# Reciprocal roots as a power on GpSimd, stores on other queues, loads in another order: one trunk layer on one core

## The chip, the cores and the metric

The kernel runs on one core of a Trainium2 chip. The metric is device time in microseconds for one execution. TensorE (PE) multiplies matrices, and PEld is its loading of stationary operands; VectorE (DVE), ScalarE (ACT) and GpSimd (POOL) do the elementwise work; SyncE (SP) issues most of the transfers between HBM and the on-chip memory. Each engine runs its own instructions in order, and engines wait for each other by semaphores.

## The reference

One layer of a gated decoder trunk, for a prompt of 1024 tokens and for 8 samples of 8 tokens (64 tokens), which share all weights. The width is 1024, all data are float32.

```python
mod = silu(c) @ ada_w + ada_b
shift, scale, gate = split(mod, 3)
h = rmsnorm(x, norm_g) * (1 + scale) + shift
z = h @ w_in + b_in                  # 1024 -> 8456 columns, split for three branches
ya = chunk_gmlp(a_u, a_v)            # branch A: rmsnorm of a_v, 128-position mixing matrices
yb = swa_branch(b_q, b_k, b_v)       # branch B: rmsnorm of q and k, window attention with sinks
yc = mlstm_branch(c_qk, c_v, ...)    # branch C: causal conv, 4 heads, chunked scan, rmsnorm of each head
merged = sum over branches of sigmoid(m_g) * ((y * silu(g)) @ w_branch)
out = x + gate * (merged @ w_out)
```

Here `rmsnorm(x, g) = x * rsqrt(mean(x*x) + 1e-6) * g`. Beside the output, the new states of branches B and C (keys, values, conv rows, the matrices C, the vectors n and m) and the normalised rows of branch A are returned.

## The kernel before, in words

Both groups of tokens are handled together as 1088 columns (prompt first, then samples), in nine tiles of 128 tokens (the last has 64) or in three chunks of 384, 384 and 320. Each float32 product is made of three matmuls on a high and a low half (`hh`, `hl`) of either operand; the halves are made by ACT (a cast) and DVE (the difference). Weights come in slabs `hl` of two halves: four pieces are loaded by SP into three buffers `raw`, cast by ACT (line 124), and subtracted by DVE (line 125), in `load_pieces`; the next slab is loaded while one is used.

The program runs through these stages, in microseconds from the span's start:

- 0 to about 90: the adaLN columns (`mod`, weights `adaraw`, results `modA` and `modB`), the root mean square of each token tile (`norm1`), the transposed and modulated activations (`hprep`), and the first products. The string LOADS sets the order of the loads on SP: x are token tiles, a the adaLN weights, w the first slab, s seven rows of biases and gains. STEPS sets the order of the work: N norms, M `mod`, S the transposed rows of s, three digits a range of `hprep` with its products, P the pieces of the next slab.
- 90 to 360: branch C, one head after the other (`head`), interleaved with gate products. A head ends with its numerator `num` scaled by a reciprocal root of nine columns (lines 744 to 752), and with stores of C from `Cst` and `Cs`.
- 360 to 612: branch B and the start of A. PE's order is written out by hand here (a manual schedule with a list of steps and filler products); other engines are ordered by the scheduler. `k_norm`, `q_stats` and `q_transpose` normalise keys and queries; `kst` and `qraw` are key and query tiles, `Sm` scores.
- 612 to 1114: the gate and branch products of half the width each, as seven products instead of eight (Strassen-like). `raw_load` brings weights, `comb` adds or subtracts them, `prod` holds their halves (lines 1372 to 1378); `t_first`, `t_second`, `t_third` and `t_in_place` make the sums of activations. Gate columns of adaLN (`graw`, line 1628) are loaded along the way.
- 1114 to 1224: the output projection; its moving operand is the weight (`wo`, the first group `prod`), its stationary one the merged activations (`mh`, `ml`).

The reciprocal root is made on DVE: an integer shift and a multiply-add for a first guess, then three Newton steps of three instructions each (`rsqrt`, lines 160 to 168); for the nine token tiles a form of two instructions each step stands in `norm1` (lines 328 to 337). Elsewhere a scaling by the number of elements stands ahead of it.

Instructions of the same engine are put in order by a scheduler that follows the program's order and priorities. SP issues loads and stores in one queue; a store or load whose semaphore isn't there yet holds what is behind it. A load also waits for an earlier one on its lane, of which there are eight.

Of the kernel before, what the change touches and what calls it, by code (L numbers as in the profile page):

```python
# [11 lines left out]
I32 = mybir.dt.int32  # L12
MAGIC = 1597463007.0
# [26 lines left out]
def trunk_kernel(ctx: ExitStack, tc: tile.TileContext, I, O):  # L40
# [12 lines left out]
    hp = ctx.enter_context(tc.tile_pool(name="hact", bufs=1))  # L53
    sp = ctx.enter_context(tc.tile_pool(name="slots", bufs=1))
# [61 lines left out]
    def load_pieces(i):  # L116
        hl = wp.tile([128, 2, 2112], F32R, tag="hl", bufs=2, name="hl")
        off = 0
        for src in [x[:, j:j + x.shape[1] // 2] for x in specs[i] for j in (0, x.shape[1] // 2)]:
# [35 lines left out]
    rsc = ct([128, 2], "rsc")  # L155
    onecol = ct([128, 1], "onecol")
    V.memset(rsc[:, 0:1], -1.0)
    V.memset(rsc[:, 1:2], MAGIC)

    def rsqrt(y, x):  # L160
        p, n = x.shape[0], x.shape[1]
        t = cp.tile([128, 20], F32, tag="rst", bufs=2, name="rst")[:p, :n]
        V.tensor_scalar(y.bitcast(I32), x.bitcast(I32), 1, None, ALU.logical_shift_right)
        V.tensor_scalar(y.bitcast(I32), y.bitcast(I32), rsc[:p, 0:1], rsc[:p, 1:2], ALU.mult, ALU.add)
        for _ in range(3):
            V.tensor_tensor(t, y, y, ALU.mult)
            V.scalar_tensor_tensor(t, t, -0.5, x, ALU.mult, ALU.mult)
            V.scalar_tensor_tensor(y, t, 1.5, y, ALU.add, ALU.mult)
# [73 lines left out]
    with tc.tile_pool(name="start", bufs=1, side="right", reuse_waits="tile") as st:  # L242
# [81 lines left out]
        def norm1(n):  # L324
            tn = TILES[n][1]
            junk = st.tile([128, 1024], F32, name="junk")
            S.activation(junk[:tn], xt[n][:tn], AF.Square, accum_out=ss[:tn, n:n + 1])
            s, y = ss[:, n:n + 1], rst[:, n:n + 1]
            V.tensor_scalar(s, s, 1.0 / 1024, EPS, ALU.mult, ALU.add)
            V.tensor_scalar(y.bitcast(I32), s.bitcast(I32), 1, None, ALU.logical_shift_right)  # L330
            V.tensor_scalar(y.bitcast(I32), y.bitcast(I32), rsc[:, 0:1], rsc[:, 1:2], ALU.mult, ALU.add)
            V.tensor_scalar(s, s, -0.5, None, ALU.mult)
            t = st.tile([128, 1], F32, tag="rs1", bufs=4, name="rs1")
            for _ in range(3):
                V.scalar_tensor_tensor(t, y, y, s, ALU.mult, ALU.mult)
                V.scalar_tensor_tensor(y, t, 1.5, y, ALU.add, ALU.mult)
            V.tensor_scalar(xt[n][:tn], xt[n][:tn], y[:tn], None, ALU.mult)

        def norm(g):
# [9 lines left out]
            V.tensor_scalar(ss[:, sl], ss[:, sl], 1.0 / 1024, EPS, ALU.mult, ALU.add)  # L349
            rsqrt(rst[:, sl], ss[:, sl])  # L350
# [5 lines left out]
        for i in (64, 96):  # L356
            V.tensor_tensor(sel, sel, ident[:, i:i + 9], ALU.add)

        def mod(j):
# [15 lines left out]
            for d in range(2):  # L375
                k = 2 * j + d
                V.tensor_scalar(modA[:, k], pc[:, 16 * d:16 * d + 9], cols[:, CADA + 8 + k:CADA + 9 + k],
# [41 lines left out]
        for step in STEPS.split():  # L419
            if step == "P":  # L420
                load_pieces(1)
# [39 lines left out]
    with tc.tile_pool(name="cph", bufs=1, side="right", reuse_waits="tile") as c1:  # L461
# [166 lines left out]
        def head(h):  # L628
# [75 lines left out]
            nc.sync.dma_start(O["C_p"][0, 0, h], Cp[:, 0:128])  # L704
# [14 lines left out]
            for b2 in range(2):  # L719
# [12 lines left out]
                nc.sync.dma_start(O["C_s"][0, bs_, h].rearrange("b d e -> d b e"), Cs[b2][:, :, 0:128])  # L732
# [15 lines left out]
            V.tensor_scalar(r2, r2, 1.0 / 128, EPS, ALU.mult, ALU.add)  # L748
            r3 = c1.tile([128, 9], F32, tag="r3", name="r3")
            rsqrt(r3, r2)  # L750
# [29 lines left out]
        nc.sync.dma_start(O["n_p"].rearrange("a b h d -> (a b h) d"), nrowo[0:4])  # L780
        nc.sync.dma_start(O["n_s"].rearrange("a b h d -> (a b h) d"), nrowo[4:36])
# [1001 lines left out]
```

## Time and profile before

| what | value |
|---|---|
| three runs | 1227.0, 1229.13 and 1229.74 us; median 1229.13 |
| profiled execution | 1225.66 us, of which the span of the profile is 1223.9 |
| mean granted clock of TensorE | 0.98 |
| instructions of DVE, of POOL | 2146, 32 |
| DMA traffic | 129.76 MB, mean 106 GB/s |

Times in the profile are from the span's start. A row of a timeline gives start, duration, engine, line, operation, tiles and shapes, and in brackets the idle time just before and what ended it. In the chain of waits a row is one link: start, duration, engine and line. SPq, DVEq and PEq are the engines' queues, "issue" is time that nothing shown explains. A matmul's duration is modelled and overlaps with the next one's, so the distance between two starts says how fast they follow each other. Matmuls are named by moving and stationary operand.

### The profile page before, as it was taken

The page shows a single profiled execution, that of the slowest core. Times are in us where ns is not written, and L with a number is a line of the kernel's source. Part 1 is how long each engine was busy: PE and PEld are TensorE (multiplying, and loading weights), DVE is VectorE, ACT ScalarE, POOL GpSimd, SP SyncE. Part 2 cuts the span into 40 slices and gives each one's busy share as a digit, 9 for nine tenths or more (in the row PEclk, how much of TensorE's full clock was granted, in tenths as well). Part 3 has the DMA queues.
Part 4 walks back from the last instruction along what each step waited for, and adds up shares of the span by engine and source line. Part 5 has one row for each costly group of instructions (what it writes and reads, how often), then busy time and mean ns, then how long its engine had stood idle before and what let it go on. Part 6 is the DMA issues. An engine that isn't in the chain of part 4 may idle for free.

```text
span 1223.9 us, 23322 instructions
## 1 busy us (share of the span) xinstructions
PE 1173.7 (96%) x8900; PEld 1124.1 (92%) x8900; DVE 820.3 (67%) x2146; ACT 485.8 (40%) x1215; POOL 17.8 (1%) x32
## 2 busy tenths in 40 slices
PE   5899999999979999999979999999999999999998
PEld 2689999999969998988878999999999999999998
DVE  4767878655568778886599885655766676668333
ACT  4443444433332266887234433333433342236000
POOL 1000000000001000000000000000000000000000
PEclk9999999999989999999979999999999999999999
DMA  9711222224122211211144246522633364466332
GB/s 328 242 47 36 72 74 70 76 86 126 54 58 67 56 40 44 67 38 59 55 119 118 75 120 201 161 80 84 177 112 110 110 171 125 126 197 190 95 91 83
DMA packets 155818, 129.76 MB, mean 106 GB/s; under 512 B 13551, under 2 KB 146311, under 8 KB 155690
## 3 DMA queue, kind: packets, MB, share of 16 engines
q1 hardware_dynamic: 155706, 128.27, 35.4%
q8 instruction: 70, 1.15, 0.4%
q14 instruction: 42, 0.34, 0.1%
HBM read 99.39 MB, written 29.82 MB: 106 GB/s over the span
## 4 chain that ended last, share of the span: by engine, by line
PE 88%; DVE 5%; SPq 3%; DMA 3%; ACT 1%; issue 1%; DVEq 0%
PE pg L85 48%; PE pk L85 23%; PE pu L85 14%; PE pk L89 2%; DMA raw<-in_w_in_dram 2%; SPq L256 1%; PE pu L89 1%; DMA xts<-in_x_sample_dram 1%; SPq L272 1%; DVE comb L1372 0%; DVE prod L1378 0%; DVE hl L125 0%; ACT hl L124 0%; DVE wo L1378 0%; DVE ml L1585 0%
## 5 line engine op out<-in xcount | busy, mean ns | idle before, releaser
L85 PE MATMUL pg<-hl,hl 128*128 128x256 f32 (+3 forms) x904 | 281.1, 311 | 0.0
L85 PE MATMUL pg<-hh,hl 128*128 128x384 f32 (+1 forms) x912 | 242.2, 340 | 1.1 <-DVE hh L399 1.1
L85 PE MATMUL pg<-hl,hh 128*128 128x256 f32 (+1 forms) x1008 | 182.9, 287 | 1.0 <-DVE zif L524 1.0
L85 PEld LDWEIGHTS pg<-hl,hl 128*128 128x128 f32 x904 | 172.1, 190 | 2.4 <-issue 1.9
L85 PEld LDWEIGHTS pg<-hh,hl 128*128 128x128 f32 x912 | 163.8, 191 | 5.3 <-DVE hh L399 2.2
L85 PEld LDWEIGHTS pg<-hl,hh 128*128 128x128 f32 x1008 | 152.9, 190 | 1.5 <-PE pg L85 1.1
L1377 ACT CAST prod<-raw 128x512 fp32r<-128x512 f32 x76 | 47.1, 620 | 125.7 <-PE pk L85 54.8
L85 PE MATMUL pg<-hh,prod 128*128 128x272 f32 x400 | 84.9, 292 | 6.8 <-ACT prod L1377 6.8
L85 PE MATMUL pk<-hh,prod 128*128 128x272 f32 x368 | 78.0, 291 | 0.0
L85 PEld LDWEIGHTS pg<-hh,prod 128*128 128x128 f32 x400 | 66.7, 191 | 7.3 <-ACT prod L1377 6.9
L1378 DVE TENSOR_TENSOR prod<-raw,prod 128x512 fp32r<-128x512 f32 x76 | 52.0, 686 | 25.2 <-ACT prod L1377 24.9
L1377 ACT CAST prod<-comb 128x512 fp32r<-128x512 f32 x64 | 39.4, 616 | 69.3 <-PE pk L85 29.5
L1502 ACT ACTIVATE tt<-tt,bh 128x272 f32<-128x272 f32 x96 | 49.9, 522 | 41.0 <-DVE tt L1475 15.8
L85 PEld LDWEIGHTS pk<-hh,prod 128*128 128x128 f32 x368 | 61.4, 191 | 1.3 <-issue 0.4
L85 PE MATMUL pk<-tc,prod 128*128 128x272 f32 x444 | 61.5, 287 | 0.0
L85 PE MATMUL pg<-yh,prod 128*128 128x272 f32 x288 | 60.0, 287 | 0.0
L85 PE MATMUL pk<-yh,prod 128*128 128x272 f32 x288 | 59.9, 287 | 0.0
L85 PEld LDWEIGHTS pk<-tc,prod 128*128 128x128 f32 x444 | 57.6, 188 | 0.9 <-DVE tt L1544 0.4
L85 PE MATMUL pg<-hl,prod 128*128 128x272 f32 x200 | 58.1, 291 | 0.0
L85 PE MATMUL pg<-tc,prod 128*128 128x272 f32 x408 | 56.5, 287 | 0.0
L85 PE MATMUL pk<-hl,prod 128*128 128x272 f32 x184 | 53.5, 291 | 0.4 <-DVE hl L825 0.4
L85 PE MATMUL pu<-hh,prod 128*128 128x272 f32 x256 | 53.5, 289 | 0.0
(521 smaller groups left out, 2626.1 us busy)
## 6 DMA issues: line engine op xcount, KB each, us to landing
raw<-in_w_in_dram SPq DMA_DIRECT2D x124, 256.0 KB
dmg<-tt SPq DMA_DIRECT2D x88, 136.0 KB
mprev<-dmg SPq DMA_DIRECT2D x64, 136.0 KB
adaraw<-in_ada_w_dram SPq DMA_DIRECT2D x16, 512.0 KB
stage<-dy SPq DMA_DIRECT2D x24, 272.0 KB
xt<-in_x_prompt_dram SPq DMA_DIRECT2D x8, 512.0 KB
graw<-in_ada_w_dram SPq DMA_DIRECT2D x16, 256.0 KB
raw<-in_w_out_dram SPq DMA_DIRECT2D x32, 128.0 KB
```

The source lines that it names most:

```text
L85: T.matmul(out, lhsT=lhsT, rhs=rhs, start=start, stop=stop)
L89: T.transpose(out, in_, ident[:k, :k])
L256: nc.sync.dma_start(raw.rearrange("p (k c) -> p k c", k=4), kv(ada_w[:, base:base + 256])[:, 4 * (q % 2):4 * (q % 2) + 4])
L272: nc.sync.dma_start(xx[:TILES[n][1]], x_p[128 * n:128 * n + 128] if n < 8 else x_s)
L1377: S.copy(t[:, 0], x)
L1378: V.tensor_tensor(t[:, 1], x, t[:, 0].bitcast(F32), ALU.subtract)
L1502: S.activation(x, x, AF.Tanh, bias=bh[:, b:b + 1], scale=0.5)
```

## The change

It does the following.

1. The reciprocal root is made by GpSimd in two instructions: a scaling with an added epsilon, and a power with exponent -0.5 (`rsqrt`). This replaces the sequence on DVE and the scaling ahead of it, for the nine token tiles, the four heads of branch C, three calls for keys, six for queries and one for branch A.
2. Stores of C, n, the conv rows, the branch C outputs (`dy<-hn`), the gates of branch B (`dsg<-zb`) and the rows of A go to GpSimd's queue; the twenty stores of attention outputs (`dy<-yo`, `dy<-ys`) to ScalarE's. They were on SP.
3. At the start the last adaLN weights (a3) are loaded ahead of the rows (s), M3 stands ahead of S, the next slab's pieces are issued after the last `modA`, and the fourth piece has a buffer of its own (`raw1`).
4. The last query tile is scaled in `q_stats` instead of `q_transpose`.
5. `t_first` moves ahead in the program and to other slots (m4, m5); gate loads `graw` are issued after the newest weight load; the `comb` buffers move to a pool of their own.
6. Two unused tiles of 64 bytes per partition shift what is allocated behind them. Together with smaller constants, the activations' tiles move down by 192 bytes, the slots and slabs by 128, and raw and prod tiles of the Strassen-like stage go elsewhere.

```diff
 LEAD = 5
-LOADS = "x0 r x1 x2 a0 w0 a1 w1 x3 x4 x5 a2 x6 x7 x8 s a3"
-STEPS = "N0 M0 010 M1 230 N1 M2 450 011 231 451 N2 S M3 670 012 671 232 452 672 P"
+LOADS = "x0 r x1 x2 a0 w0 a1 w1 x3 x4 x5 a2 x6 x7 x8 a3 s"
+STEPS = "N0 M0 010 M1 230 N1 M2 450 011 231 451 N2 M3 S 670 012 671 232 452 672 P"
...
+    ctx.enter_context(tc.tile_pool(name="shift", bufs=1)).tile([128, 16], F32, name="shift")
     sp = ctx.enter_context(tc.tile_pool(name="slots", bufs=1))
...
-            raw = wp.tile([128, 528], F32, tag="raw", bufs=3, name="raw")
+            raw = raws[q] if raws[q] is not None else wp.tile([128, 528], F32, tag="raw", bufs=3, name="raw")
...
-    rsc = ct([128, 2], "rsc")
-    V.memset(rsc[:, 0:1], -1.0)
-    V.memset(rsc[:, 1:2], MAGIC)
-
-    def rsqrt(y, x):
+    mhalf = ct([128, 1], "mhalf")
+    V.memset(mhalf, -0.5)
+
+    def rsqrt(y, x, count):
         p, n = x.shape[0], x.shape[1]
-        t = cp.tile([128, 20], F32, tag="rst", bufs=2, name="rst")[:p, :n]
-        V.tensor_scalar(y.bitcast(I32), x.bitcast(I32), 1, None, ALU.logical_shift_right)
-        V.tensor_scalar(y.bitcast(I32), y.bitcast(I32), rsc[:p, 0:1], rsc[:p, 1:2], ALU.mult, ALU.add)
-        for _ in range(3):
-            V.tensor_tensor(t, y, y, ALU.mult)
-            V.scalar_tensor_tensor(t, t, -0.5, x, ALU.mult, ALU.mult)
-            V.scalar_tensor_tensor(y, t, 1.5, y, ALU.add, ALU.mult)
+        G.tensor_scalar(x, x, 1.0 / count, EPS, ALU.mult, ALU.add)
+        G.tensor_tensor(y, x, mhalf[:p].broadcast_to([p, n]), ALU.pow)
...
             if step == "P":
-                load_pieces(1)
+                with tc.issue_after(last["m"].ins):
+                    load_pieces(1, [None] * 3 + [st.tile([128, 528], F32, name="raw1")])
...
-            nc.sync.dma_start(O["C_p"][0, 0, h], Cp[:, 0:128])
+            nc.gpsimd.dma_start(O["C_p"][0, 0, h], Cp[:, 0:128])
...
-            nc.sync.dma_start(dy[0, h], hn[h])
+            nc.gpsimd.dma_start(dy[0, h], hn[h])
...
-            V.tensor_scalar(rf, rf, 1.0 / 64, EPS, ALU.mult, ALU.add)
             r3 = bt([128, 3, 4], "r3", bufs=2)
-            rsqrt(r3.rearrange("p n h -> p (n h)"), rf)
+            rsqrt(r3.rearrange("p n h -> p (n h)"), rf, 64)
             r3s[g] = r3
+            if n0 == 6:
+                for i in range(2):
+                    qr = qraw[g][i][:64, 8].rearrange("p (h d) -> p h d", d=64)
+                    V.tensor_tensor(qr, qr, r3[:64, 2, 2 * i:2 * i + 2].unsqueeze(2).broadcast_to([64, 2, 64]), ALU.mult)
...
-                nc.sync.dma_start(dy[1, 2 * g:2 * g + 2, :, 128 * n:128 * n + 128].rearrange("f p t -> p f t"),
+                nc.scalar.dma_start(dy[1, 2 * g:2 * g + 2, :, 128 * n:128 * n + 128].rearrange("f p t -> p f t"),
...
-                nc.sync.dma_start(dsg[f, :, c0:c0 + n], z)
+                nc.gpsimd.dma_start(dsg[f, :, c0:c0 + n], z)
...
-            t = slot(("m2", "m3")[k % 2], [128, 2, HT], name="tx")
+            t = slot(("m4", "m5")[k % 2], [128, 2, HT], name="tx")
...
-        tail = {11: lambda: t_second(0), 13: lambda: t_second(1), 17: lambda: t_second(2),
+        tail = {0: lambda: t_first(0), 1: lambda: t_first(1), 2: lambda: t_first(2), 3: lambda: t_first(3), 11: lambda: t_second(0), 13: lambda: t_second(1), 17: lambda: t_second(2),
...
+    w3 = ctx.enter_context(tc.tile_pool(name="w3", bufs=1, reuse_waits="tile"))
+    w3.tile([128, 16], F32, name="shift")
...
-        nc.sync.dma_start(r.rearrange("p (k c) -> p k c", k=src.shape[1]), src)
+        newest[0] = nc.sync.dma_start(r.rearrange("p (k c) -> p k c", k=src.shape[1]), src).ins
...
-        r = w2.tile([128, 512], F32, tag="comb", bufs=3, name="comb")
+        r = w3.tile([128, 512], F32, tag="comb", bufs=3, name="comb")
...
-                nc.sync.dma_start(raw.rearrange("p (k c) -> p k c", k=2),
-                                  kv(ada_w[:, 2048 + 256 * g:2304 + 256 * g])[:, 2 * q:2 * q + 2])
+                with tc.issue_after(newest[0]):
+                    nc.sync.dma_start(raw.rearrange("p (k c) -> p k c", k=2),
+                                      kv(ada_w[:, 2048 + 256 * g:2304 + 256 * g])[:, 2 * q:2 * q + 2])
```

The other calls of `rsqrt` and the other stores change in the same way. Three places show the order. First, DVE at the start. Before, with the slab's pieces `hl<-raw`, the scaling of the sample tokens `xts`, and the adaLN columns:

```order
L337 TENSOR_SCALAR xt<-xt,rstd 128x1024
L336 SCALAR_TENSOR_TENSOR rstd<-rs_590,rstd 128x1
L335 SCALAR_TENSOR_TENSOR rs_590<-rstd,ss 128x1
L336 SCALAR_TENSOR_TENSOR rstd<-rs_590,rstd 128x1
L125 TENSOR_TENSOR hl<-raw,hl 128x528
L337 TENSOR_SCALAR xts<-xts,rstd 64x1024
L377 TENSOR_SCALAR modA<-pk,cols 128x9
L379 TENSOR_SCALAR modB<-pk,cols 128x9
L377 TENSOR_SCALAR modA<-pk,cols 128x9
L379 TENSOR_SCALAR modB<-pk,cols 128x9
```

Now:

```order
L388 TENSOR_TENSOR hl_404<-hf,hh_403 128x384
L365 TENSOR_SCALAR modA<-pk,cols 128x9
L367 TENSOR_SCALAR modB<-pk,cols 128x9
L365 TENSOR_SCALAR modA<-pk,cols 128x9
L367 TENSOR_SCALAR modB<-pk,cols 128x9
L414 COPY cols<-pk 128x52
L415 COPY cols<-pk 128x16
L124 TENSOR_TENSOR hl<-raw,hl 128x528 x3
L124 TENSOR_TENSOR hl<-raw_731,hl 128x528
```

The adaLN columns and, ten rows further ahead (row 48 of this engine), the scaling of xts stand ahead of all four pieces, one of which is in a buffer of its own.

Second, DVE at the end of branch C's last head, up to the scaling of `num`. `tc` and `tx` belong to the sums of activations for the Strassen-like stage, `rst` and `r` to the reciprocal root. Before:

```order
L125 TENSOR_TENSOR hl<-raw,hl 128x512
L166 TENSOR_TENSOR rst<-r_2986 128x9
L167 SCALAR_TENSOR_TENSOR rst<-rst,r_2982 128x9
L825 TENSOR_TENSOR tc<-tx,tc 128x544
L168 SCALAR_TENSOR_TENSOR r_2986<-rst,r_2986 128x9
L125 TENSOR_TENSOR hl<-raw,hl 128x512
L976 MEMSET qraw 64x128
L166 TENSOR_TENSOR rst<-r_2986 128x9
L167 SCALAR_TENSOR_TENSOR rst<-rst,r_2982 128x9
L168 SCALAR_TENSOR_TENSOR r_2986<-rst,r_2986 128x9
L751 TENSOR_TENSOR r_2982<-r_2986,dd 128x9
L752 TENSOR_TENSOR num<-num,r_2982 128x9x128
```

Now:

```order
L719 TENSOR_TENSOR Cs<-Cs,pk 128x4x128
L813 TENSOR_TENSOR tc<-tx,tc 128x544
L1208 TENSOR_TENSOR tx<-tx 128x544
L1206 TENSOR_TENSOR tx<-hh_312 128x544
L124 TENSOR_TENSOR hl<-raw,hl 128x512
L1207 TENSOR_TENSOR tx<-hl_313 128x544
L124 TENSOR_TENSOR hl<-raw,hl 128x512
L739 TENSOR_TENSOR r_2871<-r_2874,dd 128x9
L124 TENSOR_TENSOR hl<-raw,hl 128x512
L813 TENSOR_TENSOR tc<-tx,tc 128x544
L1208 TENSOR_TENSOR tx<-tx 128x544
L740 TENSOR_TENSOR num<-num,r_2871 128x9x128
```

The Newton steps are gone. From the second `Cs` to `num` stand nine large instructions (`tc`, `tx` and `hl`) and the small product r. Before, the slab's fourth piece is the last `hl` shown; now it stands behind `num`.

Third, SP at the beginning of the Strassen-like stage. Before:

```order
L1181 DMA dsg<-zb 128x384 x2
L1165 DMA dy<-ys 128x2x32 x2
L1181 DMA dsg<-zb 128x320
L1165 DMA dy<-ys 128x2x32
L1628 DMA graw<-in_ada_w_dram 128x2x256 x3
L1367 DMA raw_7314<-in_w_in_dram 128x4x128
L1367 DMA raw_7316<-in_w_in_dram 128x4x128
L1367 DMA raw_7318<-in_w_in_dram 128x4x128
L1628 DMA graw<-in_ada_w_dram 128x2x256
L1367 DMA raw_7320<-in_w_in_dram 128x4x128
L1367 DMA raw_7367<-in_w_in_dram 128x4x128
```

Now:

```order
L1236 DMA WT<-dWT 128x512
L1242 DMA vgb<-in_gmlp_vnorm_g_dram 64x512
L1238 DMA bsb<-in_gmlp_bs_dram 128x512
L1355 DMA raw_7086<-in_w_in_dram 128x4x128
L1355 DMA raw_7088<-in_w_in_dram 128x4x128
L1355 DMA raw_7090<-in_w_in_dram 128x4x128
L1355 DMA raw_7092<-in_w_in_dram 128x4x128
L1355 DMA raw_7139<-in_w_in_dram 128x4x128
L1355 DMA raw_7141<-in_w_in_dram 128x4x128
L1355 DMA raw_7143<-in_w_in_dram 128x4x128
L1355 DMA raw_7145<-in_w_in_dram 128x4x128
L1617 DMA graw<-in_ada_w_dram 128x2x256 x4
```

The eight weight loads stand ahead of the gate loads, and the stores of dsg and dy are on other queues.

More of the change, by code (lines that the diff above doesn't have):

```diff
@@ L327, in norm1 @@
             S.activation(junk[:tn], xt[n][:tn], AF.Square, accum_out=ss[:tn, n:n + 1])
[L328 to L336, printed above, removed]
+            y = rst[:, n:n + 1]
+            rsqrt(y, ss[:, n:n + 1], 1024)
             V.tensor_scalar(xt[n][:tn], xt[n][:tn], y[:tn], None, ALU.mult)
@@ L348, in norm @@
                 S.activation(junk[:tn], xt[n][:tn], AF.Square, accum_out=ss[:tn, n:n + 1])
-            V.tensor_scalar(ss[:, sl], ss[:, sl], 1.0 / 1024, EPS, ALU.mult, ALU.add)
-            rsqrt(rst[:, sl], ss[:, sl])
+            rsqrt(rst[:, sl], ss[:, sl], 1024)
             for n in range(3 * g, 3 * g + 3):
@@ L357, in trunk_kernel @@
             V.tensor_tensor(sel, sel, ident[:, i:i + 9], ALU.add)
+        last = {}
         def mod(j):
```

37 lines of the change are left out of this document (14 added, 23 removed).

## The prediction

> **What bounds the kernel now.** I read the page first (engine shares, then the chain of waits), then PE's own waits, then the stretches in which these fall, each by the timeline of the engine that is waited for.
>
> ```profile
> PE 1173.7 (96%) x8900; PEld 1124.1 (92%) x8900; DVE 820.3 (67%) x2146; ACT 485.8 (40%) x1215; POOL 17.8 (1%) x32
> PE 88%; DVE 5%; SPq 3%; DMA 3%; ACT 1%; issue 1%; DVEq 0%
> ```
>
> PE is busy for 1173.7 of 1223.9 us and makes 88% of the chain that ended last. So no removed DVE, SP or Pool time is worth anything by itself; it is worth what it takes from PE's idle time, from the half-clock time behind an idle stretch, or from the time of a matmul. PE's waits, largest first (us in all, times, longest):
>
> ```profile
> PE pk L89 <- DVE num L752: 8.7, 1, 8.7
> PE pg L85 <- ACT prod L1377: 6.8, 1, 6.8
> PE pk L89 <- DVE ff L543: 2.9, 1, 2.9
> PE pk L89 <- ACT kst L958: 2.3, 1, 2.3
> PE pk L89 <- DVE qraw L1007: 2.0, 1, 2.0
> PE pu L89 <- ACT Sm L1064: 1.4, 1, 1.4
> ```
>
> These add up to 24.1 us, and each stands at a place that the change touches; elsewhere nothing can be gained but by faster matmuls. Two stretches, from the start and from attention, have their uses below (columns: stretch, its length, busy time and count of PE, PEld, DVE, ACT, POOL, granted clock, DMA share, GB/s).
>
> ```profile
> 34.00:38.00 4.00, 2.60 (x26) 1.69 (x22) 2.20 (x11) 1.97 (x4) 0.00 (x0) 1.00 0.43 118
> 402.00:612.00 210.00, 201.09 (x1545) 185.24 (x1543) 156.16 (x517) 133.27 (x478) 0.00 (x0) 0.98 0.17 49
> ```
>
> **Reciprocal roots.** The change takes 258 small instructions from DVE (nine tiles of ten at the start; fourteen calls of eleven later, and the scaling ahead of each) and gives Pool 23 pairs, a scaling and a power. One of the DVE groups:
>
> ```profile
> L168 DVE SCALAR_TENSOR_TENSOR r<-rst,r 128x12 f32<-128x12 f32 (+1 forms) x30 | 5.1, 168 | 0.6
> ```
>
> At 0.17 us this is 44 of DVE's 820 us: 1.7 us for a tile of the start, 11 x 0.17 = 1.9 for a later call, in series. What a power costs on Pool, no row shows. Its nearest rows are these, a small one and a large two-input one:
>
> ```profile
> 84.27 0.19 POOL L623 TENSOR_SCALAR_AFFINE_SELECT bmask<-bmask 64x8 f32<-64x8 f32 x1
> 18.59 2.35 POOL L283 TENSOR_TENSOR hl<-raw,hl 128x1024 fp32r<-128x1024 f32 x1 [17.22 <-ACT hl L282]
> ```
>
> So a pair costs between 0.4 and 4.7 us. Its tiles have 1 to 12 columns, as the first row's have 8, so I take about 1 us, less than the 1.9 it replaces: no cost where it isn't queued behind something. Below this appears only as DVE time that others get.
>
> **The start.** SP's rows show seven small row loads ahead of the last four adaLN weights, which stand behind them for lane waits; DVE and PE follow.
>
> ```profile
> 30.44 3.04 SPq L266 DMA_DIRECT2D R<-in_b_in_dram  x4
> 38.25 2.04 SPq L256 DMA_DIRECT2D adaraw<-in_ada_w_dram  x4
> 56.32 0.71 DVE L125 TENSOR_TENSOR hl<-raw,hl 128x528 fp32r<-128x528 f32 x1 [2.07 <-ACT hl L124]
> 53.45 0.34 PE L85 MATMUL pu<-hl,hl 128*128 128x384 f32 x1
> 53.63 0.34 PE L85 MATMUL pu<-hh,hl 128*128 128x384 f32 x1
> 58.40 0.61 PE L89 MATMUL pk<-ident,xt 128*128 128x128 f32 x2 [2.94 <-DVE ff L543]
> 64.48 0.52 PE L85 MATMUL pg<-hh,hl 128*128 128x384 f32 x1
> 64.80 0.52 PE L85 MATMUL pg<-hl,hl 128*128 128x384 f32 x1
> ```
>
> DVE waits 2.07 us at 56.32 for the first weight slab's fourth piece, and the scaling of the sample tokens and the last adaLN columns, which PE needs at 58.40, are queued behind it: that is the 2.94 us wait. In the new order both stand ahead of the slab's pieces, and the piece gets a buffer of its own. The wait goes. Matmuls after it start 0.32 us apart instead of 0.18, still so at 64.8: of these 6.4 us, 6.4 x (1 - 0.18/0.32) = 2.8 are lost. The DMA share of 0.43 between 34 and 38 us, while the small rows wait for lanes, is a hole of 4 x 0.57 = 2.3 us that the earlier adaLN loads can fill. Bounds: 0 (the same idle time at another weight) and -5.7. I take the wait and half the clock: **-4.3**.
>
> **From the mLSTM heads to attention**, DVE's and SP's rows:
>
> ```profile
> 349.54 0.69 DVE L730 TENSOR_TENSOR Cs<-Cs,pk 128x512 f32<-128x512 f32 x1 [0.34 <-PE pk L85]
> 350.98 0.72 DVE L1219 TENSOR_TENSOR tx<-hh 128x544 f32<-128x544 f32 x1
> 351.62 0.72 DVE L1220 TENSOR_TENSOR tx<-hl 128x544 f32<-128x544 f32 x1
> 356.54 0.69 DVE L125 TENSOR_TENSOR hl<-raw,hl 128x512 fp32r<-128x512 f32 x1 [0.69 <-ACT hl L124]
> 358.33 1.36 DVE L752 TENSOR_TENSOR num<-num,r 128x1152 f32<-128x1152 f32 x1
> 348.82 1.81 SPq L732 DMA_DIRECT2D out_dram<-Cs  x2
> 353.05 4.58 SPq L123 DMA_DIRECT2D raw<-in_w_in_dram  x4
> ```
>
> PE waits 8.7 us for num. Most of it isn't the root: between reciprocal and num DVE runs large instructions 0.64 us apart. In the new order nine of them stand between the second Cs (which PE releases at 349.5, done 350.2) and num, so num starts at 350.2 + 9 x 0.64 + 0.2 = 356.2 instead of 358.33: **-2.1**. The piece of 356.54, late since its load stood behind two stores on SP, now comes after num. Pool has from about 349.5, when its input is ready, to 355.9 for the pair; even 4.7 us behind the issue of one Cs store (half of 1.81) fit. Bounds: 0 (a slab piece late again) and -2.8 (one more of the nine out of the way).
>
> **Attention.** Of the chain of waits, what ends PE's wait at a query transpose:
>
> ```profile
> 469.84 0.29 DVE qraw L1007
> ```
>
> The qraw scaling is moved to where the root is made, away from the transpose that waits for it: 2.0 us gone. The kst wait ends a DVE chain in which two calls are mixed; half of 2.3 goes with their small instructions. The Sm wait is ACT's, and remains. **-3.1**; bounds 0 and -5.7 (all three). The twenty stores that go to ACT's queue cost ACT some 20 x 0.4 = 8 us of issue, if as on SP above (1.81 for two being the long end); ACT is busy 133 of those 210 us, so little shows: **+0.5**, bounds 0 and +2. Stores on Pool cost PE nothing unless a pair is queued behind them (below).
>
> **From attention to the Strassen-like stage:**
>
> ```profile
> 619.90 1.40 SPq L1628 DMA_DIRECT2D graw<-in_ada_w_dram  x3
> 621.34 1.68 SPq L1367 DMA_DIRECT2D raw<-in_w_in_dram  x3
> 625.96 0.62 ACT L1377 CAST prod<-raw 128x512 fp32r<-128x512 f32 x1 [1.24 <-DMA raw<-in_w_in_dram]
> 621.93 0.71 DVE L1517 TENSOR_TENSOR tx<-hh,hh 128x544 f32<-128x544 f32 x1
> 626.79 0.69 DVE L1378 TENSOR_TENSOR prod<-raw,prod 128x512 fp32r<-128x512 f32 x1
> ```
>
> PE waits 6.8 us for weights whose load went out at 621.34, behind gate loads that wait for PE. The new order has these loads first, and their tiles no longer share space with what PE reads until 619.9. DVE is next: prod stands there after three in-place instructions from 621.93, at 621.93 + 3 x 0.64 = 623.9 instead of 626.79: **-2.9**. Bounds: 0 and -6.8 (PE begins with the cast half at once).
>
> **Addresses.** In the last stage 24 matmuls of one shape (128x256), with stationary operands mh and ml, take, by the chain of waits:
>
> ```profile
> 1128.15 2.72 PE pg L85 x24
> 1151.93 2.81 PE pk L85 x24
> 1197.36 2.87 PE pg L85 x24
> 399.95 1.79 PE pg L85 x15
> ```
>
> 113.3, 117.1 and 119.6 ns each: with the moving operand in prod, and in two places of wo. From the tiles' addresses prod stands 192 bytes past the stationary ones, counted modulo 256, the last group 0. The projections with 256 columns (fourth row, 119.3 ns) stand at 128 before and at 192 after, as the pools move by 192 and 128 bytes. There are 1248 of them:
>
> ```profile
> L85 PE MATMUL pg<-hl,hh 128*128 128x256 f32 x864 | 156.8, 287 | 0.0
> L85 PE MATMUL pg<-hl,hl 128*128 128x256 f32 x384 | 109.0, 284 | 0.0
> ```
>
> If the distance is the cause, 1248 x 5.2 ns = 6.5 us; only prod shows the fast rate, so I take half: **-3.2**, bounds +1.3 (its 240 matmuls lose it: 240 x 5.6 ns) and -6.5. The Trainium skill (TensorE: Matmul & The Clock Gate, section Back-to-back issue gap) gives columns / 2.4 + 2.5 ns, 109.2 ns here by that page's estimate, whatever the address; the rows are all above it and differ. By that rule the term is nothing, which is the first rival.
>
> **Sum.** -4.3 - 2.1 - 3.1 + 0.5 - 2.9 - 3.2 = -15.1 us. The profiled execution took 1225.66 (span 1223.9), 3.5 below the median of the runs shown, 1229.13. That gives 1210.6 by the profiled one and **1214.0** by the median.
>
> **Rivals.** *Addresses do nothing*: the rest is -11.9, 1217.2. For it: only one tile shows the fast rate, which may have another reason. Against: the same shape keeps three rates for 24 matmuls after 24. *Everything comes*: -5.7 - 2.8 - 5.7 - 6.8 - 6.5 = -27.5, 1201.6. Against it: behind each load DVE is the next to be late, and its large instructions remain. *No change*: at both transitions and at the start the same DVE work stays ahead of PE and only the qraw wait goes, 1227.1; against it, the orders quoted do put fewer instructions ahead. *Slower: Pool is in order, and its pairs come late.* Each pair waits for its predecessor and for stores ahead of it, and DVE's scaling, with all that is queued behind it, waits for the pair. At 4.7 us a pair, the six tiles of the start that follow the first three take 6 x (4.7 - 1.7) = 18 us more, and nine calls in attention 9 x (4.7 - 1.9) = 25. With -15.1 that is +28, 1257. It is 15 us for each us over 1.8, so it decides from 1.8 + 15.1/15 = 2.8 us a pair. For it: nothing of the trace shows Pool at such work, and Pool's 2.35 us. Against: that row has 1024 columns. The Trainium skill (SBUF — State Buffer, section SBUF: two separate sides) speaks for it: a store issued from GpSimd can take about 3.1 us instead of 0.62 while VectorE holds the shared port. No run here shows that.
>
> **How the numbers follow.** Forecast 0.45; addresses nothing 0.20; everything 0.12; no change 0.10; slower 0.13. The likeliest own range is 1207 to 1220. The range from 1198 to 1230 leaves out the slower case and the ends of two others, under 2 in 10; its low end is the second rival with the clock at the start of attention regained as well. A measurement of this kernel can tell about 0.2% (2.5 us) from no change: faster 0.78, the same 0.09, slower 0.13.
>
> **What would show it.** The ff wait gone and 384-column matmuls 0.18 us apart by 62 us; num 2 us earlier after its reciprocal, its wait still over 5 us; no qraw wait; the first prod wait near 4 us; projections at 113 to 119 ns. Wrong: Pool pairs over 2 us, PE waiting for DVE instructions that read them, or projections above 119.3.

## The result and the profile after

The changed kernel takes 1214.6 us (median of four runs, 1212.79 to 1217.25); the kernel before took 1229.06 in the same comparison (1227.0 to 1229.74). The ratio is 0.9887, with a 95% interval from 0.9862 to 0.9912. The forecast of 1214.0 us is met in total, but not term by term.

The profiled execution of the changed kernel took 1217.25 us, the longest of its four; that of the kernel before, 1225.66, is shorter than its runs in this comparison. So the two traces show only 8.4 of the 14.5 us between the medians. The profile of a second set of runs of the changed kernel (a1_again below, 1215.79 us) is used beside it.

The shares of the engines and the chain of waits, changed kernel:

```profile
PE 1166.3 (96%) x8900; PEld 1116.6 (92%) x8900; DVE 787.7 (65%) x1887; ACT 485.4 (40%) x1215; POOL 76.9 (6%) x111
PE 53%; DVE 3%; ACT 3%; DMA 1%; issue 1%; SPq 0%; ACTq 0%; DVEq 0%
```

PE is still the bound and busy 7.4 us less with the same 8900 instructions, so its matmuls became faster. The shares of this chain add up to far under 100% (it breaks off), so it isn't compared with the 88% of before. DVE lost 259 instructions and 32.6 us of busy time (the forecast's 44 took each small instruction at its full duration), which by itself is worth nothing here. PE's waits (us in all, times, longest), changed kernel:

```profile
PE pk L84 <- DMA adaraw<-in_ada_w_dram: 7.5, 5, 6.1
PE pk L88 <- DVE num L740: 6.3, 1, 6.3
...
PE pk L84 <- ACT msb L355: 3.6, 3, 2.2
PE pg L84 <- DVE prod L1366: 3.0, 1, 3.0
...
PE pg L84 <- ACT prod L1365: 2.4, 1, 2.4
PE pk L84 <- DVE QT L1006: 2.1, 1, 2.1
PE pu L88 <- ACT Sm L1051: 1.7, 1, 1.7
PE pk L84 <- ACT hh L812: 1.6, 1, 1.6
...
PE pk L88 <- DVE QT L1006: 1.5, 1, 1.5
...
PE pk L84 <- DVE hl L813: 1.0, 1, 1.0
```

Of the six waits that the forecast listed, ff, kst and qraw are gone and num is 2.4 us shorter. The prod wait of 6.8 us is now two, on ACT and on DVE, of 5.4 together. New or longer are the waits for QT (2.1 and 1.5), hh (1.6), hl (1.0, before 0.4) and msb (3.6, before 1.6).

The forecast's list left out three rows of before that its order would include: th (5.7), ots (2.5) and one at the roots that the change moves, where PE waits for `rstd` ahead of its first adaLN products:

```profile
PE pk L85 <- DVE rstd L336: 5.2, 1, 5.2
```

In the changed kernel this wait is the 6.1 us of the first row above, put down to the load that came last. It takes 4.6 to 6.2 us in all fourteen profiles, whichever engine makes the roots. So nothing was gained there. th (now 5.8) and ots are as before.

Milestones on PE show the stages. They are the starts of matmuls in each profiled execution, in us from the start of the span: *start ends*, the first transposes for the first head's gates; *heads end*, the transposes of the last head's num; *attention ends*, the last query transposes; *sums mixed*, the last transposes of mixed spatial weights; *inner stage*, the last product with the gate rows ahead of the Strassen-like stage's steady part; *its end*, the stage's last product; *end*, the last product with the output weights.

| | before | e1 | e12 | after | a1 | e3 | e6 | e9 |
|---|---|---|---|---|---|---|---|---|
| start ends | 105.4 | 107.1 | 107.8 | 105.9 | 105.1 | 103.1 | 105.3 | 105.5 |
| heads end | 361.7 | 361.8 | 356.7 | 357.9 | 357.1 | 361.8 | 352.6 | 352.5 |
| attention ends | 539.0 | 537.0 | 533.0 | 529.9 | 529.4 | 536.7 | 525.8 | 527.3 |
| sums mixed | 619.6 | 617.1 | 612.6 | 608.9 | 606.7 | 617.3 | 603.1 | 604.9 |
| inner stage | 688.5 | 685.8 | 682.2 | 680.4 | 679.3 | 688.1 | 672.4 | 677.0 |
| its end | 1118.2 | 1116.7 | 1112.8 | 1110.9 | 1109.8 | 1119.2 | 1102.9 | 1107.6 |
| end | 1220.0 | 1217.2 | 1215.4 | 1211.5 | 1210.0 | 1219.5 | 1203.4 | 1209.2 |

From before to after the start gains nothing. The heads take 252.0 us instead of 256.3, attention 172.0 instead of 177.3. The entry of the Strassen-like stage, from "sums mixed" to "inner stage", takes 71.5 us instead of 68.9: longer, where the forecast had it 2.9 shorter.

### The profile page after: what moved, and what is told of

Read it like the earlier page. It is cut to its first block, busy times and chain, and to the rows that moved or that the text cites. A ratio compares the mean times of both kernels' runs of the same rounds, so it can differ in the third digit from the quotient of the medians.

```text
span 1215.5 us, 23135 instructions
## 1 busy us (share of the span) xinstructions
PE 1166.3 (96%) x8900; PEld 1116.6 (92%) x8900; DVE 787.7 (65%) x1887; ACT 485.4 (40%) x1215; POOL 76.9 (6%) x111
## 4 chain that ended last, share of the span: by engine, by line
PE 53%; DVE 3%; ACT 3%; DMA 1%; issue 1%; SPq 0%; ACTq 0%; DVEq 0%
PE pg L84 21%; PE pk L84 18%; PE pu L84 12%; ACT vn L1254 1%; DMA raw<-in_w_in_dram 0%; ACT Sm L1043 0%; DMA raw<-in_w_out_dram 0%; PE pu L88 0%; DVE prod L1366 0%; DVE sA L1264 0%; ACT hl L123 0%; ACT Sm L1051 0%; DVE ml L1573 0%; DVE tx L1219 0%; DVE wo L1366 0%
## 5 line engine op out<-in xcount | busy, mean ns | idle before, releaser
L84 PE MATMUL pg<-hl,hh 128*128 128x256 f32 (+1 forms) x1008 | 179.1, 285 | 0.2 <-ACT pg L1193 0.2
L84 PEld LDWEIGHTS pg<-tc,prod 128*128 128x128 f32 x408 | 54.1, 191 | 0.4 <-issue 0.4
```

Source lines behind the costliest of these rows:

```text
L84: T.matmul(out, lhsT=lhsT, rhs=rhs, start=start, stop=stop)
```

## The experiments

Each ratio is to the kernel before on the same chip, with its 95% interval.

### Addresses: e1_shift_alone, e8_shift_192, e2_no_shift, a1_again

The theory is that the distance between the two operands of a matmul sets its rate, so that 64 bytes alone shorten the kernel. The rival is that they do nothing. e1 is the kernel before with one line; e8 has the same line with 48 columns, 192 bytes:

```
     hp = ctx.enter_context(tc.tile_pool(name="hact", bufs=1))
+    ctx.enter_context(tc.tile_pool(name="shift", bufs=1)).tile([128, 16], F32, name="shift")
     sp = ctx.enter_context(tc.tile_pool(name="slots", bufs=1))
```

e2 is the changed kernel without that line and without `w3.tile([128, 16], F32, name="shift")`. a1 is the changed kernel, beside them on their chip.

> Before, with one unused tile of 64 bytes ahead of the slots and nothing else. Addresses decide: token projections (256 columns) start 115 ns apart instead of 118.8, the 384-column matmuls 173.4 instead of 176.0, the output projection's first 208 matmuls 119 instead of 113.5: -4.2 - 2.4 + 0.5 = -6 us, 1223. Addresses do nothing: the same distances as before and 1229.

> Before, with an unused tile of 192 bytes ahead of the slots: token projections at 64, 384 columns at 192, the output projection's wo at 192 and prod at 128. If 192 is the fast distance for every shape: 384 columns below 173 ns (936 of them, at least -3 us), wo at 113.5 instead of 119.4 (-2.1), token projections 117.5 (-1.5), prod 119 (+1.1): 1223.5 or less. If only the 256-column shape knows a distance: 384 columns as before, 1226.5. If addresses do nothing: 1229.

> The changed kernel without its two unused tiles of 64 bytes, so that weights and activations stand 128 bytes apart modulo 256 again, as before. Addresses decide: matmuls as slow as before (118.8 and 176.0 ns), 6 us slower than the changed kernel, 1220.5. Addresses do nothing: 1214.6.

> The changed kernel once more. Both theories: 1214.6 us, 0.988 to 0.990 of before. What it tells apart: in the first profile PE waited 7.5 us for the last adaLN weights at the start, and the start brought nothing. If that belongs to the order of the loads, a second profile shows such a wait again, over 5 us. If it belongs to that execution, the wait is under 2 us here and the start is 3 to 5 us shorter.

| | median us (runs) | ratio | interval |
|---|---|---|---|
| before | 1227.52 (15) | 1 | |
| e1_shift_alone | 1221.15 (6) | 0.9941 | 0.9923 to 0.9960 |
| e8_shift_192 | 1223.46 (10) | 0.9956 | 0.9936 to 0.9976 |
| e2_no_shift | 1220.8 (4) | 0.9940 | 0.9921 to 0.9959 |
| a1_again | 1215.93 (4) | 0.9900 | 0.9880 to 0.9921 |

The shift alone is worth 6.4 us, and the changed kernel loses 4.9 without it. The question in the expectation of a1 comes out neither way: the wait put down to adaraw is 1.5 us in all there, but the start is only 0.8 us shorter (105.1 for 105.9). The 6.1 us of the first profile were no wait for the last adaLN weights: in a1 the same products wait 5.6 us, put down to DVE's `xt`.

The projections with 256 columns, grouped by form (busy us, mean ns of one; the matmuls overlap), in the changed kernel:

```profile
L84 PE MATMUL pg<-hl,hh 128*128 128x256 f32 x864 | 153.4, 285 | 0.2 <-ACT pg L1193 0.2
```

in e1:

```profile
L86 PE MATMUL pg<-hl,hh 128*128 128x256 f32 x864 | 154.0, 286 | 0.0
...
1124.67 2.88 PE pg L86 x24
```

and in e2:

```profile
L83 PE MATMUL pg<-hl,hh 128*128 128x256 f32 x864 | 156.2, 287 | 0.0
...
1123.37 2.72 PE pg L83 x24
```

The same 864 matmuls are busy 153.4 and 154.0 us with the shift and 156.2 without, as 156.8 before. The second rows are from the chain of waits: 24 matmuls with prod at the beginning of the output stage, 120.0 ns each in e1 and 113.3 in e2. So the shift costs time at that place and gives time to the projections. Clearer is the distance from one start to the next, the mean over consecutive matmuls of one shape and pair of tiles, idle gaps left out (ns; by the distance in bytes, modulo 256, from the next matmul's stationary operand to the moving one, worked out from the addresses that the program gives to the tiles):

| | 0 | 64 | 128 | 192 |
|---|---|---|---|---|
| projections, 256 columns | | 115.9 (e8) | 118.7 (before), 118.7 (e2) | 115.4 (after), 115.5 (e1) |
| projections, 384 columns | | 173.4 (after), 173.4 (e1) | 176.0 (before), 176.0 (e2) | 174.7 (e8) |
| output stage, prod with mh | 120.0 (e1) | 118.0 (after) | 118.8 (e8) | 113.6 (before), 113.7 (e2) |
| output stage, wo with mh | 119.2 (before) | 117.8 (after) | 118.9 (before) | 116.4 (after), 117.6 (e8) |

Every group changes with the distance, in kernels that otherwise keep their work. It is the distance and not the place: in e2 both operands of the projections stand 64 bytes further, modulo 256, than before, and the rates are those of before. No one distance is best for every shape: at 192 the 384-column projections are slower than at 64, and wo doesn't reach prod's 113.6. Projections with 320 columns do not change (146.5 to 147.0 ns at 64, 128 and 192). In the changed kernel this gives 1248 x 3.3 ns = 4.1 us for the 256-column projections and 936 x 2.6 = 2.4 for the 384-column ones; prod gives back 0.9 (208 x 4.4) and wo gains 0.7. That is 6.3 us; measured are 4.9 against e2, where the intervals of the two ratios leave some 3 us on either side, and 6.4 in e1, where prod gives back more. For e8 the same sum is 1248 x 2.8 + 936 x 1.3 - 208 x 5.2 + 363 x 1.6 = 4.2, beside 4.1 measured. The rival falls. The Trainium skill's formula (TensorE: Matmul & The Clock Gate, section Back-to-back issue gap), which has no term for addresses and gives 109.2 ns for 256 columns, doesn't describe these rows (113.6 to 120.0); the page itself gives it for an isolated matmul. What in the chip does this isn't shown.

### Reciprocal roots: e12_roots_alone, e3_roots_on_dve

e12 is the kernel before with only the roots changed; e3 is the changed kernel with the roots back on DVE (for the token tiles too in the general form of `rsqrt`):

```
-        G.tensor_scalar(x, x, 1.0 / count, EPS, ALU.mult, ALU.add)
-        G.tensor_tensor(y, x, mhalf[:p].broadcast_to([p, n]), ALU.pow)
...
+        V.tensor_scalar(x, x, 1.0 / count, EPS, ALU.mult, ALU.add)
+        V.tensor_scalar(y.bitcast(I32), x.bitcast(I32), 1, None, ALU.logical_shift_right)
+        V.tensor_scalar(y.bitcast(I32), y.bitcast(I32), rsc[:p, 0:1], rsc[:p, 1:2], ALU.mult, ALU.add)
+        for _ in range(3):
...
```

> Before, with the reciprocal roots on GpSimd and nothing else of the change. If the roots pay by themselves (num's wait 8.7 to near 2, attention 2.4 shorter, the start 1 to 2 longer): -7 to -8, 1219.5. If they pay only together with the early sums, which the roots on VectorE made dearer: -3, 1224, and num's wait over 6.

> The changed kernel with the reciprocal roots back on VectorE (a shift, a multiply-add and three Newton steps), the queues, orders and addresses of the change kept. If the roots pay by what they take from VectorE ahead of num, kst and qraw: num's wait is back near 8 us, the kst or qraw waits of about 2 us are back, 1219 us. If the stores on other queues did it: 1215, with num's wait near 6.3.

e12 took 1220.46 us (4 runs; before 1225.87): 0.9951, from 0.9935 to 0.9968. e3 took 1224.25 (10 runs; before 1226.97): 0.9971, from 0.9958 to 0.9984, where the changed kernel has 0.9887 and 0.9900. So the roots on Pool are worth 0.5% alone and about 0.8% within the change. They and the shift together (0.49% and 0.59%) make up what the whole change brings (1.0 to 1.1%); by this addition everything else nets to nothing that the intervals can tell. The matmul rates of e12 are those of before (118.7 and 176.1 ns for the projections), so its gain isn't one of addresses.

The waits of PE show where. e12:

```profile
PE pk L89 <- DVE num L737: 2.1, 1, 2.1
```

and e3:

```profile
PE pk L90 <- DVE num L749: 12.5, 1, 12.5
...
PE pk L90 <- ACT kst L954: 2.0, 1, 2.0
PE pk L90 <- DVE qraw L997: 2.0, 1, 2.0
```

The num wait falls from 8.7 to 2.1 with the roots alone, and the heads take 248.9 us instead of 256.3. From the second `Cs` to num there are 2.6 us in e12 and 8.8 before: the nine large instructions that stood between them are three. The Newton steps had each waited for a turn between large instructions; without them num is queued ahead of six of these. Within the change the num wait is 12.5 without the Pool roots and 6.3 with them. The qraw and kst waits, which the forecast gave to the moved scaling and the mixed calls, are both back in e3, where the scaling is moved all the same, and both absent in e12, where it isn't: the shorter root removes them. Yet attention takes 176.3 us in e12 and 177.3 before, so the roots alone shorten this stage by 1.1 us, not by the 4.3 us of the two waits (PE waits 1.9 us for `Sm` there instead). What the pairs cost on Pool, changed kernel, by groups (the last three columns are busy us, mean ns, idle before):

```profile
L162 POOL TENSOR_TENSOR r<-rr,mhalf 128x12 f32<-128x12 f32 x6 | 14.2, 2370 | 0.5
...
L162 POOL TENSOR_TENSOR rstd<-ss,mhalf 128x1 f32<-128x1 f32 x9 | 5.5, 612 | 0.8
L162 POOL TENSOR_TENSOR kr<-kr,mhalf 128x6 f32<-128x6 f32 x3 | 4.0, 1332 | 0.2
...
L161 POOL TENSOR_SCALAR rr<-rr 128x12 f32<-128x12 f32 x6 | 2.2, 364 | 109.7 <-ACT Sm L1043 55.4 <-DVE es L1049 21.0 <-DVE rr L980 19.8
```

### The order at the end: e6_end_as_before, e9_sums_late

e9 is the changed kernel with one thing put back, the time and place of the first part of the activation sums (`t_first`):

```
-            t = slot(("m4", "m5")[k % 2], [128, 2, HT], name="tx")
+            t = slot(("m2", "m3")[k % 2], [128, 2, HT], name="tx")
...
-        tail = {0: lambda: t_first(0), 1: lambda: t_first(1), 2: lambda: t_first(2), 3: lambda: t_first(3), 11: lambda: t_second(0), ...
+        tail = {11: lambda: t_second(0), ...
...
+            if n in (1, 3, 5, 7):
+                t_first(n // 2)
```

e6 puts back this and also the place of the comb tiles (w2) and the order of the gate loads (no `issue_after`).

> The changed kernel with the sums of activations, the comb buffers and the gate loads at the beginning of the Strassen-like stage as before. If VectorE is what that stage waits for, so that earlier weights only move the wait: between 1213 and 1215.5, the first prod wait near 6 us again and the waits on hh and hl gone. If the loads' order brought the predicted 2.9 us: 1218.

> The changed kernel with only the first sums of activations (t_first) back in their old place and slots; the comb pool and the gate loads' order stay as changed. If the early sums cost what they put ahead of num: num's wait about 2 us, as with the whole end undone, and 1211 if the order of loads at the Strassen-like stage is worth nothing, 1208 if it is worth the 2.9 us predicted. If something else of the end was the cost: num's wait 6.3 and 1215.

e6 took 1210.86 us (4 runs; before 1226.97): 0.9861, from 0.9832 to 0.9891. e9 took 1212.18 (4 runs; before 1225.87): 0.9881, from 0.9863 to 0.9898. Neither was compared with the changed kernel directly; their ratios are below its 0.9887 and 0.9900, with intervals that overlap. The stage is clear: the heads take 247.3 and 247.0 us, and 252.0 in both profiles of the changed kernel. DVE's rows there in the changed kernel:

```profile
348.23 0.68 DVE L719 TENSOR_TENSOR Cs<-Cs,pk 128x512 f32<-128x512 f32 x1
348.83 0.72 DVE L813 TENSOR_TENSOR tc<-tx,tc 128x544 fp32r<-128x544 f32 x1
349.46 0.72 DVE L1208 TENSOR_TENSOR tx<-tx 128x544 f32<-128x544 f32 x1
...
352.57 0.16 DVE L739 TENSOR_TENSOR r<-r,dd 128x9 f32<-128x9 f32 x1
352.65 0.68 DVE L124 TENSOR_TENSOR hl<-raw,hl 128x512 fp32r<-128x512 f32 x1
353.25 0.72 DVE L813 TENSOR_TENSOR tc<-tx,tc 128x544 fp32r<-128x544 f32 x1
353.89 0.72 DVE L1208 TENSOR_TENSOR tx<-tx 128x544 f32<-128x544 f32 x1
354.52 1.35 DVE L740 TENSOR_TENSOR num<-num,r 128x1152 f32<-128x1152 f32 x1
```

and in e6:

```profile
347.51 0.69 DVE L719 TENSOR_TENSOR Cs<-Cs,pk 128x512 f32<-128x512 f32 x1 [0.75 <-PE pk L84]
348.11 0.72 DVE L813 TENSOR_TENSOR tc<-tx,tc 128x544 fp32r<-128x544 f32 x1
348.75 0.17 DVE L739 TENSOR_TENSOR r<-r,dd 128x9 f32<-128x9 f32 x1
...
350.14 1.35 DVE L740 TENSOR_TENSOR num<-num,r 128x1152 f32<-128x1152 f32 x1
```

From the second Cs to num there are 6.3 us in the one and 2.6 in the other: tc and tx of the early sums, with the slab's pieces, are queued ahead of num. The num wait is 2.1 us in e6 as in e9. So the roots take 7.4 us from the heads and the early sums return 4.7. Part of this comes back in attention, which takes 173.1 us in e6 and 174.8 in e9, but 172.0 with the sums made earlier. What the early sums cost the whole kernel lies between nothing and some 5 us by these ratios.

In e6 the load order at the Strassen-like stage is the old one as well, and PE waits there as before; the same view of e6:

```profile
PE pg L84 <- ACT prod L1367: 6.9, 1, 6.9
```

Yet from "sums mixed" to "inner stage" e6 takes 69.3 us, the changed kernel 71.5. The shorter first wait is given back. PE in the changed kernel, with the idle time and what ended it:

```profile
611.61 0.40 PE L84 MATMUL pg<-hh,prod 128*128 128x272 f32 x1 [2.42 <-ACT prod L1365]
615.16 0.82 PE L84 MATMUL pg<-hh,prod 128*128 128x272 f32 x2 [3.03 <-DVE prod L1366]
638.12 0.39 PE L84 MATMUL pk<-hh,prod 128*128 128x272 f32 x1 [1.59 <-ACT hh L812]
639.50 0.40 PE L84 MATMUL pk<-hl,prod 128*128 128x272 f32 x1 [0.99 <-DVE hl L813]
```

and the same stretch by windows (columns as in the forecast):

```profile
600.00:620.00 20.00, 12.01 (x69) 11.11 (x69) 19.21 (x44) 7.22 (x19) 0.54 (x1) 0.75 0.05 12
620.00:640.00 20.00, 17.41 (x137) 16.99 (x136) 19.45 (x37) 8.42 (x16) 0.00 (x0) 1.00 0.47 132
```

DVE is busy 19.2 and 19.5 of 20 us. PE starts on prod sooner, but DVE's other work for this stage isn't done sooner, and PE then waits at 615 us for DVE's prod and at 638 us for hh and hl, both made from `tx`, which DVE finishes at 637.4.

The second pair of waits seems to cost more than its 2.6 us, by the clock that follows it. In the 15 us that begin 30 us after "sums mixed" the granted clock is 0.89 in the changed kernel and 0.78 in a1, and 1.00 in the six kernels with the old order of loads, which take 68.7 to 69.8 us for this stage. Seven of the eight kernels with the new order have a clock of 0.78 to 0.89 there and take 70.1 to 72.6; the eighth, e11, has no hh wait (hl 1.3 us), a clock of 1.00, and takes 68.5. So even where the clock holds, the new order gains little here.

### Stores and start: e4_stores_on_sp, e5_start_as_before

e4 issues all moved stores from SP again, eleven lines of this kind:

```
-            nc.gpsimd.dma_start(O["C_p"][0, 0, h], Cp[:, 0:128])
+            nc.sync.dma_start(O["C_p"][0, 0, h], Cp[:, 0:128])
```

e5 has LOADS, STEPS and the first slab's pieces as before (`... a3 s` to `... s a3`, `M3 S` to `S M3`, `load_pieces(1)` without a buffer of its own).

> The changed kernel with all stores back on SyncE's queue. If the roots pay: 1215 and num's wait near 6.3. If the stores held the weight loads on that queue: num's wait is near 8 and the time 1218.

> The changed kernel with the order of loads and steps at the start as before, and no buffer of its own for the fourth piece. If the start is bound by the transfers and the wait only moved (ff 2.9 before, msb 2.2 to 2.8 now): 1215, a wait of about 3 us on ff again, the first gate matmuls (zif) within 1 us of 105.5. If the order brought what was predicted, hidden by the spread of the transfers: 1219, and zif 3 us later.

e4 took 1216.87 us (4 runs): 0.9908, from 0.9886 to 0.9931; e5 took 1217.39 (4 runs): 0.9922, from 0.9894 to 0.9951; before 1226.97 for both. Neither differs from the changed kernel's 0.9887 and 0.9900 by more than the intervals: the queues of the stores are worth nothing that can be measured, the order at the start between nothing and 0.3%. With the stores on SP, num waits 6.0 us in place of 6.3, and attention takes 170.5 us in place of 172.0, so the forecast's +0.5 for ACT's stores is not refuted. In e5, with the old order, the start ends at 107.1 us and PE's ff wait doesn't come back, nor is it there in e12, where PE waits 4.1 us for msb instead: the roots on Pool are enough to remove it. At the start the changed kernel's SP, PE and ACT show this:

```profile
32.54 7.07 SPq L250 DMA_DIRECT2D adaraw<-in_ada_w_dram  x4
...
57.89 1.06 PE L84 MATMUL pk<-sel,msb 128*128 128x9 f32 x8 [2.19 <-ACT msb L355]
...
65.64 0.52 PE L84 MATMUL pg<-hh,hl 128*128 128x384 f32 x1
65.96 0.52 PE L84 MATMUL pg<-hl,hl 128*128 128x384 f32 x1
...
55.57 0.63 ACT L123 CAST hl<-raw 128x528 fp32r<-128x528 f32 x1 [0.86 <-DMA raw<-in_w_in_dram]
56.72 0.63 ACT L123 CAST hl<-raw 128x528 fp32r<-128x528 f32 x1 [0.52 <-DMA raw<-in_w_in_dram]
57.26 0.58 ACT L355 COPY msb<-pk 128x512 f32<-128x512 f32 x1
```

The issue of the adaLN loads begins 5.7 us earlier, but takes 7.07 us instead of 2.04 and so ends only 0.7 us earlier. PE now waits 2.19 us for ACT's msb at 57.89, in place of 2.94 for ff at 58.40, and its matmuls stand 0.32 us apart at 65.6, as before. The ACT rows show why the wait only moved. The slab's pieces no longer stand ahead of the adaLN columns on DVE, but their casts stand ahead of msb on ACT, and the last two wait for their loads. Before, ACT made msb at 52.10 us, ahead of the fourth cast at 55.66:

```profile
52.10 0.58 ACT L367 COPY msb<-pk 128x512 f32<-128x512 f32 x1
55.66 0.63 ACT L124 CAST hl<-raw 128x528 fp32r<-128x528 f32 x1 [2.98 <-DMA raw<-in_w_in_dram]
```

The order is that of before in the three kernels that have an ff wait of 2.9 to 3.5 us (before, e1 and e8), and msb stands behind the fourth cast in the eleven others.

### The token tiles' roots: e10_end_undone_start_roots_dve, e11_sums_late_start_roots_dve

e10 is e6, and e11 is e9, with the token tiles' roots at the start on DVE (the removed lines of `norm1` put back, `rsqrt` elsewhere on Pool). The question was whether Pool costs time at the start, as e3's 103.1 us for it beside 105.9 and 105.1 suggests.

> The end as before, and the roots of the nine token tiles back on VectorE; the later roots stay on GpSimd. If GpSimd's roots make the start longer, as the one profile with them on VectorE had it (first gate matmuls at 103.1 instead of 105.4 us): 1208.5, and zif near 103. If that was the spread of the transfers: 1211.

> Both: sums late, loads at the Strassen-like stage as changed, roots of the token tiles on VectorE. If the loads' order there is worth 2.9 us and the start 2.4: 1206. If neither: 1211.

e10 took 1209.99 us (5 runs; before 1225.87): 0.9875, from 0.9854 to 0.9895; e11 took 1211.93 (5 runs): 0.9881, from 0.9862 to 0.9899. The start ends at 107.7 and 105.6 us, not near 103. So this isn't confirmed. The start differs by about 2 us between kernels that are alike there (107.7 in e10, 105.6 in e11); what 103.1 came from stays open. One thing differs between 20 and 34 us: the granted clock is 0.99 to 1.00 in five of the six kernels with these roots on DVE (0.76 in e11), and 0.54 to 0.80 in six of the eight with them on Pool (0.74 in the changed kernel; 1.00 in e6 and 0.98 in e9). That the roots cause it isn't shown. Of all the kernels, e6 and e10 are nominally the fastest, 1.5 to 5 us under the changed kernel by ratio, less than their intervals can tell apart.

## Why the forecast was right in total, and where its terms were wrong

| term (us) | forecast | measured in the stages |
|---|---|---|
| start | -4.3 | +0.5 (a1 -0.3) |
| heads to attention | -2.1 | -2.6 |
| attention, with ACT's stores | -2.6 | -3.2 |
| entry of the Strassen-like stage | -2.9 | +2.6 (a1 +3.7) |
| addresses (from the rates) | -3.2 | -6.3 |
| sum | -15.1 | -9.0 |

The heads' stage shrinks by 4.3 us, of which 1.7 are addresses (1.6 in e1, 1.9 between e2 and the change); attention by 5.3, of which some 2.1 are addresses (e1). The rows do not divide the profile up: the start still holds its share of the addresses, and the stages not listed change by -2.0 together. The profiles differ by 8.4 us, a1's by 9.9; the medians by 14.5 and 11.6. The rest lies in runs of one kernel that differ by 3 to 8 us.

- **Roots.** That they are worth only DVE time that others get was right, and so was it that no PE wait is for a Pool pair itself. But "most of it isn't the root" was wrong at num: the roots alone take 6.6 of its 8.7 us. The step that failed took the large instructions between the reciprocal and num as fixed; six of nine stood there because num's root was not ready (e12). A pair was taken at about 1 us and is 0.9 (0.31 + 0.61) to 2.7 (0.36 + 2.37). So the sign "Pool pairs over 2 us" did show, for the heads and the queries, and the largest is near the 2.8 us from which the slower rival decides. That rival didn't come: the new waits of PE (QT, hh, hl and msb) aren't for instructions that read a pair, the pairs in the heads and attention lie beside other DVE work, and the nine of the start are of the shortest kind.
- **Heads to attention.** -2.6 against -2.1, and num starts 2.5 us earlier after its Cs (6.3 against 8.8 us), its wait over 5 us, as forecast. The reason was two effects that were not told apart: -7.4 from the roots, +4.7 from the early sums, which the forecast counted among the nine instructions but not as a loss.
- **Attention.** Right in size (-3.2 for -2.6) and in the waits that went: no qraw and no kst wait, the Sm wait remains. It is the root, not the moved scaling, that removes them (e3, e12). But waits for QT of 3.6 us came in their place, and e12 without the two waits is only 1.1 us shorter; so a wait gone was not time gone, and the size was in part luck: the early sums, which the forecast didn't count here, shorten the stage by 1.1 to 2.8 us (e6, e9). Without ACT's stores it is 1.5 us shorter in e4's one profile, where 0.5 was forecast.
- **Entry of the Strassen-like stage.** Wrong. That the first wait falls was right (2.4 us, then 3.0 on DVE; near 4 was forecast). The step that failed is the end of the sum there: PE's gain at the first prod was counted as time, though DVE, busy 19 of each 20 us, sets the next 30 us, and a lower clock (0.89) follows the waits of 2.6 us at 638 us.
- **Start.** Wrong. The ff wait goes, but the wait moves to msb and the half clock stays. The step that failed looked at the queue of DVE alone: the slab's pieces are cast on ACT, where they now stand ahead of msb. Not gained either was the 5.2 us wait for the first roots, which the forecast's list left out. The sign "384 columns 0.18 us apart by 62 us" didn't come. The lower bound, "the same idle time at another weight", is what came.
- **Addresses.** The mechanism was right and mis-sized, -3.2 for -6.3. Each 256-column matmul gains 3.3 ns, not 5.2 (nor the 6.0 that the four rows shown there give, 119.3 less 113.3); 208 matmuls, not 240, use prod here; but half was taken for doubt, and the 384-column matmuls, put at nothing, gain 2.4 us. The rival "addresses do nothing" falls.

The two wrong terms overstate by 4.8 and 5.5 us, addresses and attention understate by 3.1 and 0.6: the total is nearer than its parts deserve. That 1214.0 was met within 1 us is luck: the medians of the second comparison differ by 11.6 us, not 15.1.

## What to carry to other kernels

Where PE is the bound and DVE is nearly full ahead of a transition, price a removed or an added DVE instruction by everything that is queued ahead of the one PE waits for; a few us of early work placed there take back what small instructions gave. When work is moved out of one engine's queue, look where its pieces stand in the queue of the engine before it. An earlier load is worth something only if the engine behind the load has room too: look at its busy share in the stretch after the wait. When a few hundred matmuls of one shape show different steady rates in different places, compare the addresses of their operands: a shift by 64 bytes was the cheapest gain here.

## What was not expected of the hardware

The steady rate of matmuls of 256 and 384 columns depends on the distance of their operands in memory modulo 256 bytes: 113.3 to 120.0 ns and 173.4 to 176.0 ns, with 128 the slowest for both kinds of projection and 0 the slowest with prod; 320 columns show nothing (146.5 to 147.0). The same distance doesn't give one rate for all tiles (115.4 ns with the projections, 113.6 with prod, at 192). A power on Pool grows with the columns: 0.61 us for 1, 1.33 for 6, 1.83 for 9, 2.37 for 12, much dearer than the scaling (0.2 to 0.36). The instruction that issues a store takes Pool 0.5 to 0.8 us here, in a stage (that of the C stores) in which DVE is busy 168 of 255 us:

```profile
L721 POOL DMA_DIRECT2D out_dram<-Cs x8 | 6.3, 784 | 37.6 <-DVE Cs L627 9.0 <-DVE Cs L719 8.4 <-DVE cso L462 7.8
```

The 3.1 us of the Trainium skill (SBUF — State Buffer, section SBUF: two separate sides) are for a whole transfer beside a copy on DVE that holds the shared port. Whether such a copy ran beside one of these stores isn't shown.
